# An encoder in split float32 products: streamed operands and low weights get start places of their own

## The chip, the cores and the metric

The kernel runs on one core of a Trainium2 chip. The metric is the device time of one execution in microseconds (us); smaller is better. Engines are named as in the profile: PE is the matrix engine (TensorE) and PEld its weight loads, DVE is VectorE, ACT is ScalarE, POOL is GpSimd, and SP issues DMAs.

## The reference

The kernel computes two layers of an encoder on 16 learned and 256 input tokens (272 together) of width 2048. All tensors are float32. Cut to what matters:

```python
for i in range(DEPTH):                                   # 2 layers
    h = _rmsnorm(h_stream, norm_mix[i])
    proj = h @ w_in[i]                                   # 2048 -> q 1024, k 256, v 256, f 1024, gates 2 x 2048
    ...                                                  # q, k: per-head norm and rotary; sigmoid of the gates
    a_br = attn @ w_attn_br[i]                           # 8 heads of 128, 2 key/value heads -> 2048
    s_br = fr.reshape(B, L, FOURIER_WIDTH) @ w_four[i]   # real part of a 2-D DFT of f -> 2048
    merged = g_attn * a_br + g_four * s_br
    h_stream = h_stream + merged @ w_out[i]
    h2 = _rmsnorm(h_stream, norm_ffn[i])
    up = h2 @ w_up[i]                                    # 2048 -> gate 5632 and value 5632
    u_gate = _dwconv3_centred(up[..., :D_FF], w_conv[i], b_conv[i])
    h_stream = h_stream + (jax.nn.silu(u_gate) * up[..., D_FF:]) @ w_down[i]
return h_stream[:, N_META:]
```

## The kernel before

Activations lie transposed: 128 channels across the partitions, the tokens along the row. Every large product is made of three matmuls in a reduced float32 format: an operand x is kept as a high half (x rounded) and a low half (x minus the high half), weights likewise, and the sum is high weights times high x, high weights times low x, low weights times high x. In the function `group` these are L248, L249 and L250, in this order, each with a 128 x 128 block of weights that is loaded anew, and the tokens as the stream. A stream has 272 columns in layer 0. In layer 1 some tokens are not needed any more: most streams have 258 columns (`lo` is 14), those of the up-value and down products 256 (`lo2` is 16). There two streams of 256 fit one result buffer, so high and low x go through in a single instruction of 512 columns (L244), followed by low weights times high x with 256 (L245); the last group of the last down product is done in the three-matmul form.

`order` is a list of all products by key (layer, kind, number): f, k, v, q (input projections), ga, gf (gates), s (Fourier branch), a (attention branch), o (output), ug and uv (the up product's gate and value half), d (down). Each product's weights come in chunks of 4 x 2 blocks, 512 KB, through SP's queue into `raw`, four buffers. `split_w` makes of each chunk the high weights `wh` on ACT (L193) and the low weights `wl` on DVE (L196), three buffers each. `group` asks for chunks two ahead; the work of the other engines is written between the matmuls by `step` and `pump`. The tile framework adds the semaphores.

Streams come from few tiles: `xHL` (the normalised residual, 16 rows of channels, high and low beside each other), `qH` and `qL`, `mH` and `mL` (the gated sum that goes to `w_out`), and `gHL` (the FFN's inner activations). Their rows are 320 words long (`XP`), more than the 272 in use, and the tokens begin at a word that the table in L50 gives, by tile and layer:

```python
X_AT, Q_AT, G_AT = (8, 24), (24, 40), (40, 48)
```

The high and the low half of a tile begin at the same word. In this text the place of an operand is the number of its first 4-byte word within its partition, modulo 64, as the built program lays it out; words skipped by `lo` count. Since 320 is five times 64, it is the same for all rows of a tile. Before the change:

| products | stream | place, high and low | place of `wh`, `wl` |
|---|---|---|---|
| layer 0: f, k, v, q, ga, gf, a, o, ug, uv, d | 272 | 8, 8 | 32, 32 |
| layer 1: f, k, v | 272 | 24, 24 | 32, 32 |
| layer 1: q, ga, gf, a, o, ug | 258 | 38, 38 | 32, 32 |
| layer 1: uv | 512 and 256 | 40, 40 | 32, 32 |
| layer 1: d | 512 and 256 | 32, 32 | 32, 32 |

Of the kernel before, what the change touches and what calls it, by code (L numbers as in the profile page):

```python
# [11 lines left out]
F32R = mybir.dt.float32r  # L12
# [4 lines left out]
P = 128  # L17
# [3 lines left out]
T = NM + SEQ  # L21
# [3 lines left out]
NH = 8  # L25
# [7 lines left out]
CW = 4  # L33
MG = 2
FF_SPLIT = (24, 20)
PRE = 26
XP = 320
# [9 lines left out]
HC = 64  # L47
HC1 = HC + 1
TH = T // 2 + 2
X_AT, Q_AT, G_AT = (8, 24), (24, 40), (40, 48)  # L50
BLK = ((0, 16), (16, 144), (144, 272))

C_COS, C_SIN, C_MASK = 0, T, 2 * T
# [58 lines left out]
def encoder_kernel(ctx, tc, xT, params, consts, bmat, w_in, w_abr, w_four, w_f64, w_out, w_up, w_down, outT):  # L112
    nc = tc.nc
    per = ctx.enter_context(tc.tile_pool(name="per", bufs=1))
    wp = ctx.enter_context(tc.tile_pool(name="wp", bufs=3))
# [4 lines left out]
    order = []  # L120
# [25 lines left out]
            k0 += n  # L146
    chunks = [ch for _, chs in order for ch in chs]
    folded = {i for i, k in enumerate(k for k, chs in order for _ in chs) if k[1] == "s"}
    st = {"raw": 0, "fetch": 0, "next": 0, "grp": 0}
    raws, splits, behind = {}, {}, {}  # L150
    RAW, LOOK = 4, 2
# [34 lines left out]

    def split_w(i, a, b, eng=None):
        if i not in splits:
            splits[i] = tuple(wp.tile([P, CW, MG * P], F32R, tag=t, name=f"{t}{i}") for t in ("wh", "wl"))
        h, lo = splits[i]  # L190
        r = raws[i]
        if eng is None:
            nc.scalar.copy(h[:, a:b], r[:, a:b])  # L193
        else:
            eng.tensor_copy(h[:, a:b], r[:, a:b])
        nc.vector.tensor_tensor(lo[:, a:b], r[:, a:b], h[:, a:b].bitcast(F32), op=ALU.subtract)  # L196
        if b == CW:
            del raws[i]
# [185 lines left out]
    nc.gpsimd.memset(remO, 0.0)  # L384

    def xs(k, half, lo=0, l=0):
        return xHL[:, k, half, X_AT[l] + lo:X_AT[l] + T]

    cos = cst[:, C_COS:C_COS + T]
    sin = cst[:, C_SIN:C_SIN + T]  # L390
# [58 lines left out]
    for l in range(DEPTH):  # L449
        last = l == DEPTH - 1  # L450
        lo = 14 if last else 0
# [5 lines left out]
        with tc.tile_pool(name=f"mix{l}", bufs=1) as mp:  # L457
            x64 = mp.tile([96, TH], F32R, name="x64")
            E = mp.tile([P, NH, XP], F32, tag="q1", name="E")[:, :, 0:T]
            qL = mp.tile([P, NH, XP], F32R, name="qL")[:, :, Q_AT[l]:Q_AT[l] + T]  # L460
            AHn = 3 * 4 * T
            ALn = 8 * XP
            o1Hf = mp.tile([P, AHn], F32R, tag="aH", name="o1H")
# [233 lines left out]
            cnt = [0]  # L697
            for pn in pns:
                nc.gpsimd.memset(pn[:, 0:P], 0.0)
            qH = mp.tile([P, NH, XP], F32R, tag="q1", name="qH")[:, :, Q_AT[l]:Q_AT[l] + T]  # L700

            def q_stage(i, qp, qsq):
                kv, j = i // 2, i % 2
# [147 lines left out]
            for half in range(2):  # L851
                mH = mL = None
                for kind, i in BRANCH_ORDER[half]:
                    j = i - 4 * half
                    if kind == "ga":
                        tha[i] = gate("ga", i)
                    elif kind == "gf":
                        w64s.append(split_w64(l, i))
                        thf[i] = gate("gf", i)
                    elif kind == "s":  # L860
                        def s_evac(m, ps, th=thf[i]):
                            e, o = (mp.tile([P, TH], F32, tag=t, name=t) for t in ("se", "so"))
                            for a, p_ in ((e, ps[0]), (o, ps[1])):
                                nc.scalar.copy(a, p_[:, TH:2 * TH])
                                nc.vector.tensor_tensor(a, p_[:, :TH], a, op=ALU.add)
                            sp = mp.tile([P, T], F32, tag="sp", name="sp", bufs=2)
                            nc.vector.tensor_tensor(sp[:, 0:TH], e, o, op=ALU.add)
                            nc.vector.tensor_tensor(sp[:, TH:T], e[:, T - TH:0:-1], o[:, T - TH:0:-1], op=ALU.subtract)
                            t_ = th[:, m, lo:T]
                            nc.vector.scalar_tensor_tensor(t_, t_, 1.0, sp[:, lo:T], op0=ALU.add, op1=ALU.mult)  # L870

                        four_group((l, "s", i), fr, x64, w64s.pop(0), s_evac)
                    else:
                        if mH is None:
                            drain()
                            mHf = mp.tile([P, AHn], F32R, tag="aH", name="mH")
                            mLf = mp.tile([P, ALn], F32R, tag="aL", name="mL")
                            mH, mL = (t_[:, :8 * XP].rearrange("p (k t) -> p k t", k=8)[:, :, Q_AT[l]:Q_AT[l] + T] for t_ in (mHf, mLf))
                        ps = group((l, "a", i), lambda kt: (qH[:, kt, lo:T], qL[:, kt, lo:T]), W)
                        for m in range(MG):  # L880
                            k = 2 * j + m
                            t_, h_ = tha[i][:, m, lo:T], mH[:, k, lo:T]
                            nc.vector.scalar_tensor_tensor(t_, t_, 1.0, ps[m][:, :W], op0=ALU.add, op1=ALU.mult)
                            nc.vector.tensor_tensor(t_, t_, thf[i][:, m, lo:T], op=ALU.add)
                            nc.scalar.copy(h_, t_)
                            nc.vector.tensor_tensor(mL[:, k, lo:T], t_, h_.bitcast(F32), op=ALU.subtract)
                for mg in range(8):
                    ps = group((l, "o", half, mg), lambda kt: (mH[:, kt, lo:T], mL[:, kt, lo:T]), W)
                    for m in range(MG):
                        mt = 2 * mg + m  # L890
                        nc.vector.scalar_tensor_tensor(XT[:, mt, lo:T], ps[m][:, :W], 0.5, XT[:, mt, lo:T], op0=ALU.mult, op1=ALU.add)
                        if half == 1:
                            norm_in(mt, P_NF + l * KT)


        with tc.tile_pool(name=f"ffn{l}", bufs=1) as fp:
            hold = {}
            push(norm_stats(hold), 8)
            fused = 2 * W2 <= 512
            k0 = 0  # L900
            for c, n in enumerate(FF_SPLIT):
                gHL = fp.tile([P, FF_SPLIT[0], 2, XP], F32R, tag="gHL", name="gHL")[:, :, :, G_AT[l]:G_AT[l] + T]
                gH, gL = gHL[:, :, 0, :], gHL[:, :, 1, :]
                for i in range(k0 // MG, (k0 + n) // MG):
                    ps = group((l, "ug", i), xr(lo), W)
                    drain()
                    cs = []
                    for m in range(MG):
                        mt = 2 * i + m
                        wc = lambda t: prm[:, P_CW + (l * 3 + t) * FT + mt:P_CW + (l * 3 + t) * FT + mt + 1]  # L910
                        bc = prm[:, P_CB + l * FT + mt:P_CB + l * FT + mt + 1]
                        u = fp.tile([P, T], F32, tag="u", name="u", bufs=3)
                        nc.vector.tensor_tensor(u[:, lo:T], ps[m][:, :W], rstdB[:, lo:T], op=ALU.mult)
                        cv = fp.tile([P, T], F32, tag="cv", name="cv", bufs=4)
                        nc.scalar.activation(cv[:, lo2:T], u[:, lo2:T], AF.Identity, bias=bc, scale=wc(1))
                        a = max(lo2, 1)
                        nc.vector.scalar_tensor_tensor(cv[:, a:T], u[:, a - 1:T - 1], wc(0), cv[:, a:T], op0=ALU.mult, op1=ALU.add)
                        nc.vector.scalar_tensor_tensor(cv[:, lo2:T - 1], u[:, lo2 + 1:T], wc(2), cv[:, lo2:T - 1], op0=ALU.mult, op1=ALU.add)
                        nc.scalar.activation(cv[:, lo2:T], cv[:, lo2:T], AF.Silu)
                        nc.vector.tensor_tensor(cv[:, lo2:T], cv[:, lo2:T], rstdB[:, lo2:T], op=ALU.mult)  # L920
                        cs.append(cv)
                    ps = group((l, "uv", i), (lambda kt: (xHL[:, kt, :, X_AT[l] + lo2:X_AT[l] + T],)) if fused else xr(lo2), W2)
                    for m in range(MG):
                        j = 2 * i + m - k0
                        cv = cs[m]
                        val = ps[m][:, :W2]
                        if fused:
                            v = fp.tile([P, W2], F32, tag="v", name="v", bufs=2)
                            nc.scalar.copy(v, ps[m][:, W2:2 * W2])
                            nc.vector.tensor_tensor(v, v, val, op=ALU.add)  # L930
                            val = v
                        nc.vector.tensor_tensor(cv[:, lo2:T], cv[:, lo2:T], val, op=ALU.mult)
                        nc.scalar.copy(gH[:, j, lo2:T], cv[:, lo2:T])
                        nc.vector.tensor_tensor(gL[:, j, lo2:T], cv[:, lo2:T], gH[:, j, lo2:T].bitcast(F32), op=ALU.subtract)
                lastc = c == len(FF_SPLIT) - 1
                for mg in range(8):
                    two = fused and not (lastc and mg == 7)
                    ps = group((l, "d", c, mg), (lambda kt: (gHL[:, kt, :, lo2:T],)) if two
                               else (lambda kt: (gH[:, kt, lo2:T], gL[:, kt, lo2:T])), W2)
                    for m in range(MG):  # L940
                        mt = 2 * mg + m
# [62 lines left out]
```

## Time and profile before

| | |
|---|---|
| median of 3 runs | 2562.33 us (2560.87 to 2563.58) |
| the profiled execution | 2561.68 us, of which the span is 2559.8 us |
| granted clock of TensorE | 0.999 of full speed |
| PE busy | 2552.6 us, 19732 matmuls |
| DVE, ACT busy | 1690.4 us, 1211.4 us |
| DMA | 465 MB, 182 GB/s |

Matmuls overlap, and their ends are modelled: one of 272 columns is shown as 285 ns long, although the next one starts well before. What counts is the step from one start to the next. It is had from the count of matmuls in a stretch of time in which only one kind runs, or from the start times in the timeline. In a row of the windows the numbers are: the stretch, its length, PE's busy time with the count, the granted clock, the share of DMA, and GB/s. A count takes in the two matmuls that began before the stretch and still run at its start. In the timeline a row has start and length in us, then engine, line, operation, result and operands, shape. A group's row has its count, its busy time, the mean length in ns, and the idle time ahead of it.

### The profile page before, as it was taken

What the parts mean: (1) busy time and instruction counts of PE and PEld (TensorE: products, weight loads), DVE (VectorE), ACT (ScalarE), POOL (GpSimd) and SP (SyncE); (2) the same over time, 40 slices, a digit from 0 to 9 for tenths busy, and PEclk for the clock granted to TensorE, in tenths of its full rate; (3) what the DMA queues carried; (4) which work ended last, traced back from release to release, by engine and by line L of the source; (5) the groups of instructions that cost most, each with busy time, mean ns of one, the idle gap of its engine ahead of it and who ended that gap; (6) DMA issues with size and microseconds to landing.
All of it is one profiled execution on the core that took longest, in us unless ns stands there. A gap on an engine that the chain in (4) does not pass through costs nothing.

```text
span 2559.8 us, 47859 instructions
## 1 busy us (share of the span) xinstructions
PE 2552.6 (100%) x19732; PEld 2494.2 (97%) x19732; DVE 1690.4 (66%) x2691; ACT 1211.4 (47%) x1741; POOL 18.3 (1%) x37
## 2 busy tenths in 40 slices
PE   9999999999999999999999999999999999999999
PEld 9999999999999999999999999999999998999988
DVE  7687767766565446655566878677766665566654
ACT  6455434554444334444444555345554543455443
POOL 0000000000000000000000000000000000000000
PEclk9999999999999999999999999999999999999999
DMA  7555656555555555555554546666555556655565
GB/s 236 166 153 166 192 183 189 185 175 179 180 176 181 177 178 181 175 181 178 177 172 153 174 150 199 192 199 191 184 186 189 185 187 190 189 188 186 186 202 160
DMA packets 132011, 465.34 MB, mean 182 GB/s; under 512 B 15312, under 2 KB 19280, under 8 KB 131792
## 3 DMA queue, kind: packets, MB, share of 16 engines
q1 hardware_dynamic: 127424, 457.37, 56.5%
q10 hardware_dynamic: 4368, 4.92, 0.6%
q8 instruction: 154, 2.52, 0.4%
q14 instruction: 65, 0.53, 0.1%
HBM read 457.35 MB, written 2.10 MB: 179 GB/s over the span
## 4 chain that ended last, share of the span: by engine, by line
PE 98%; DVE 1%; DMA 0%; ACT 0%; issue 0%; SPq 0%; DVEq 0%; ACTq 0%
PE ps_ug L249 7%; PE ps_ug L248 7%; PE ps_ug L250 7%; PE ps_uv L244 6%; PE ps_d L244 6%; PE ps_d L249 4%; PE ps_d L250 4%; PE ps_d L248 4%; PE ps_uv L248 3%; PE ps_uv L249 3%; PE ps_uv L250 3%; PE ps_uv L245 3%; PE ps_d L245 3%; PE ps_o L249 2%; PE ps_o L248 2%; PE ps_gf L248 2%
## 5 line engine op out<-in xcount | busy, mean ns | idle before, releaser
L196 DVE TENSOR_TENSOR wl<-raw,wh 128x1024 fp32r<-128x1024 f32 (+1 forms) x835 | 1016.8, 1220 | 697.3 <-ACT wh L193 692.4
L193 ACT CAST wh<-raw 128x1024 fp32r<-128x1024 f32 (+1 forms) x834 | 871.3, 1047 | 994.4 <-PE ps_ug L249 159.5
L248 PE MATMUL ps_ug<-xHL,wh 128*128 128x272 f32 (+1 forms) x1408 | 399.6, 284 | 0.0
L249 PE MATMUL ps_ug<-xHL,wh 128*128 128x272 f32 (+1 forms) x1408 | 399.0, 283 | 0.0
L250 PE MATMUL ps_ug<-xHL,wl 128*128 128x272 f32 (+1 forms) x1408 | 399.0, 283 | 0.0
L248 PEld LDWEIGHTS ps_ug<-xHL,wh 128*128 128x128 f32 x1408 | 264.2, 188 | 0.9
L249 PEld LDWEIGHTS ps_ug<-xHL,wh 128*128 128x128 f32 x1408 | 264.2, 188 | 0.1
L250 PEld LDWEIGHTS ps_ug<-xHL,wl 128*128 128x128 f32 x1408 | 264.1, 188 | 0.0
L244 PE MATMUL ps_uv<-xHL,wh 128*128 128x512 f32 x704 | 245.0, 390 | 0.0
L244 PE MATMUL ps_d<-gHL,wh 128*128 128x512 f32 x664 | 230.3, 391 | 0.0
L249 PE MATMUL ps_d<-gHL,wh 128*128 128x272 f32 (+1 forms) x744 | 212.0, 285 | 0.0
L248 PE MATMUL ps_d<-gHL,wh 128*128 128x272 f32 (+1 forms) x744 | 212.0, 285 | 0.0
L250 PE MATMUL ps_d<-gHL,wl 128*128 128x272 f32 (+1 forms) x744 | 212.0, 285 | 0.0
L248 PE MATMUL ps_uv<-xHL,wh 128*128 128x272 f32 x704 | 200.6, 285 | 0.0
L249 PE MATMUL ps_uv<-xHL,wh 128*128 128x272 f32 x704 | 200.6, 285 | 0.0
L250 PE MATMUL ps_uv<-xHL,wl 128*128 128x272 f32 x704 | 200.6, 285 | 0.0
L245 PE MATMUL ps_uv<-xHL,wl 128*128 128x256 f32 x704 | 198.5, 282 | 0.0
L245 PE MATMUL ps_d<-gHL,wl 128*128 128x256 f32 x664 | 185.9, 280 | 0.0
L244 PEld LDWEIGHTS ps_uv<-xHL,wh 128*128 128x128 f32 x704 | 132.1, 188 | 26.9
L244 PEld LDWEIGHTS ps_d<-gHL,wh 128*128 128x128 f32 x664 | 124.2, 187 | 27.2
L248 PE MATMUL ps_ga<-xHL,wh 128*128 128x272 f32 (+1 forms) x512 | 147.5, 288 | 0.0
L248 PE MATMUL ps_gf<-xHL,wh 128*128 128x272 f32 (+1 forms) x512 | 146.3, 286 | 0.0
(284 smaller groups left out, 5891.7 us busy)
## 6 DMA issues: line engine op xcount, KB each, us to landing
raw<-in_w_up SPq DMA_DIRECT2D x352, 512.0 KB, 3.5
raw<-in_w_in SPq DMA_DIRECT2D x207, 512.0 KB, 3.6
raw<-in_w_down SPq DMA_DIRECT2D x176, 512.0 KB, 3.5
raw<-in_w_out SPq DMA_DIRECT2D x64, 512.0 KB, 3.5
raw<-in_w_four SPq DMA_DIRECT2D x32, 512.0 KB, 3.7
raw<-in_w_abr SPq DMA_DIRECT2D x32, 512.0 KB, 3.5
qs<-qp ACTq DMA_DIRECT2D x32, 68.0 KB, 4.1
outT<-ot ACTq DMA_DIRECT2D x16, 128.0 KB, 4.0
```

Source lines behind the costliest of these rows:

```text
L193: nc.scalar.copy(h[:, a:b], r[:, a:b])
L196: nc.vector.tensor_tensor(lo[:, a:b], r[:, a:b], h[:, a:b].bitcast(F32), op=ALU.subtract)
L244: nc.tensor.matmul(o2, h[:, c, sl], ab, start=kt == 0, stop=False)
L245: nc.tensor.matmul(o, lo[:, c, sl], ab[:, 0, :], start=False, stop=kt == nk - 1)
L248: nc.tensor.matmul(o, h[:, c, sl], a, start=kt == 0, stop=False)
L249: nc.tensor.matmul(o, h[:, c, sl], b, start=False, stop=False)
L250: nc.tensor.matmul(o, lo[:, c, sl], a, start=False, stop=kt == nk - 1)
```

## The change

The start words become pairs, one for the high and one for the low half, by tile and layer. The low weights get a tile that is 64 words longer, and for the down product of both layers they begin 16 words into it. The fused streams of layer 1 (L244) now read two stretches that need not be 320 words apart: in uv they are 296 words apart. The program's instructions, their order on every engine and their waits stay as they are; only addresses, and the distance between the two parts of that fused stream, differ.

```diff
-X_AT, Q_AT, G_AT = (8, 24), (24, 40), (40, 48)
+X_AT, Q_AT, G_AT = ((4, 28), (24, 0)), ((20, 44), (40, 16)), ((12, 28), (0, 0))
+WL_AT = {(0, "d"): 16, (1, "d"): 16}
...
+    wl_at = [WL_AT.get(k[:2], 0) for k, chs in order for _ in chs]
...
     def split_w(i, a, b, eng=None):
         if i not in splits:
-            splits[i] = tuple(wp.tile([P, CW, MG * P], F32R, tag=t, name=f"{t}{i}") for t in ("wh", "wl"))
+            h = wp.tile([P, CW, MG * P], F32R, tag="wh", name=f"wh{i}")
+            lo = wp.tile([P, CW * MG * P + 64], F32R, tag="wl", name=f"wl{i}")
+            o = wl_at[i]
+            splits[i] = h, lo[:, o:o + CW * MG * P].rearrange("p (c m) -> p c m", c=CW)
...
     def xs(k, half, lo=0, l=0):
-        return xHL[:, k, half, X_AT[l] + lo:X_AT[l] + T]
+        return xHL[:, k, half, X_AT[l][half] + lo:X_AT[l][half] + T]
...
-            qL = mp.tile([P, NH, XP], F32R, name="qL")[:, :, Q_AT[l]:Q_AT[l] + T]
+            qL = mp.tile([P, NH, XP], F32R, name="qL")[:, :, Q_AT[l][1]:Q_AT[l][1] + T]
...
-            qH = mp.tile([P, NH, XP], F32R, tag="q1", name="qH")[:, :, Q_AT[l]:Q_AT[l] + T]
+            qH = mp.tile([P, NH, XP], F32R, tag="q1", name="qH")[:, :, Q_AT[l][0]:Q_AT[l][0] + T]
...
-                            mH, mL = (t_[:, :8 * XP].rearrange("p (k t) -> p k t", k=8)[:, :, Q_AT[l]:Q_AT[l] + T] for t_ in (mHf, mLf))
+                            mH, mL = (t_[:, :8 * XP].rearrange("p (k t) -> p k t", k=8)[:, :, o:o + T] for t_, o in zip((mHf, mLf), Q_AT[l]))
...
+            def both(t_, k, at):
+                a, n = at[0] + lo2, XP + at[1] - at[0]
+                if n == XP:
+                    return t_[:, k, :, a:a + W2]
+                return t_[:, k].rearrange("p r n -> p (r n)")[:, a:a + 2 * n].rearrange("p (r n) -> p r n", r=2)[:, :, :W2]
...
-                gHL = fp.tile([P, FF_SPLIT[0], 2, XP], F32R, tag="gHL", name="gHL")[:, :, :, G_AT[l]:G_AT[l] + T]
-                gH, gL = gHL[:, :, 0, :], gHL[:, :, 1, :]
+                gHL = fp.tile([P, FF_SPLIT[0], 2, XP], F32R, tag="gHL", name="gHL")
+                gH, gL = (gHL[:, :, e, G_AT[l][e]:G_AT[l][e] + T] for e in range(2))
...
-                    ps = group((l, "uv", i), (lambda kt: (xHL[:, kt, :, X_AT[l] + lo2:X_AT[l] + T],)) if fused else xr(lo2), W2)
+                    ps = group((l, "uv", i), (lambda kt: (both(xHL, kt, X_AT[l]),)) if fused else xr(lo2), W2)
...
-                    ps = group((l, "d", c, mg), (lambda kt: (gHL[:, kt, :, lo2:T],)) if two
+                    ps = group((l, "d", c, mg), (lambda kt: (both(gHL, kt, G_AT[l]),)) if two
```

The places that come of it:

| products | stream | place, high and low | place of `wh`, `wl` |
|---|---|---|---|
| layer 0: f, k, v, q, ga, gf, a, o, ug, uv | 272 | 4, 28 | 32, 32 |
| layer 0: d | 272 | 44, 60 | 32, 48 |
| layer 1: f, k, v | 272 | 24, 0 | 32, 32 |
| layer 1: q, ga, gf, a, o, ug | 258 | 38, 14 | 32, 32 |
| layer 1: uv | 512 and 256 | 40, 16 | 32, 32 |
| layer 1: d | 512 and 256 | 48, 48 | 32, 48 |

## Prediction, made before the run

> **What bounds the kernel now.** I read the page's busy line first, then the chain that ended last, then who waited for whom on TensorE.
>
> ```profile
> span 2559.8 us, 47859 instructions
> PE 2552.6 (100%) x19732; PEld 2494.2 (97%) x19732; DVE 1690.4 (66%) x2691; ACT 1211.4 (47%) x1741; POOL 18.3 (1%) x37
> PE 98%; DVE 1%; DMA 0%; ACT 0%; issue 0%; SPq 0%; DVEq 0%; ACTq 0%
> PE ps_f L304 <- ACT wh L193: 1.8, 2, 0.9
> PE ps_idle L364 <- DVE ones L360: 1.1, 1, 1.1
> ```
>
> TensorE is the whole chain (98%), and its longest wait on anything sums to 1.8 us. Nothing can be hidden better here: the time is the number of matmuls times the step from one start to the next. The busy durations do not show that step, because matmuls overlap. I take it from counts in pure windows and from start times.
>
> ```profile
> 560.00:800.00 240.00, 240.00 (x1948) 1.00 0.57 178
> 820.00:940.00 120.00, 120.00 (x975) 1.00 0.56 177
> 1772.00:1812.00 40.00, 40.00 (x339) 1.00 0.58 183
> 2090.00:2210.00 120.00, 120.00 (x694) 1.00 0.61 191
> ```
>
> These are stretches of one stage each, TensorE alone: length, busy time, count, granted clock, DMA share, GB/s. Two of each count had begun before the window. Layer 0's up products (first row) step by 240/1946 = 123.3 ns, and its down product by 120/973 = 123.3, both at 272 columns. Layer 1's output product (third row, 258 columns) steps by 40/337 = 118.7. Layer 1's down product (fourth row) issues a 512-column and a 256-column stream in turn: 120/346 = 346.8 ns a pair. The granted clock is 1.00 throughout.
>
> Now start times, for stages too short or too mixed for a window.
>
> ```profile
> 1999.63 0.28 PE L249 MATMUL ps_ug<-xHL,wh 128*128 128x258 f32 x1
> ...
> 2001.19 0.28 PE L250 MATMUL ps_ug<-xHL,wl 128*128 128x258 f32 x1
> 1383.74 0.29 PE L248 MATMUL ps_v<-xHL,wh 128*128 128x272 f32 x1
> ...
> 1384.88 0.29 PE L248 MATMUL ps_v<-xHL,wh 128*128 128x272 f32 x1
> 2547.73 0.28 PE L248 MATMUL ps_d<-gHL,wh 128*128 128x256 f32 x1
> ...
> 2550.97 0.28 PE L248 MATMUL ps_d<-gHL,wh 128*128 128x256 f32 x1
> 1899.89 0.39 PE L244 MATMUL ps_uv<-xHL,wh 128*128 128x512 f32 x1
> 1900.12 0.28 PE L245 MATMUL ps_uv<-xHL,wl 128*128 128x256 f32 x1
> 1900.23 0.39 PE L244 MATMUL ps_uv<-xHL,wh 128*128 128x512 f32 x1
> ...
> 1900.93 0.39 PE L244 MATMUL ps_uv<-xHL,wh 128*128 128x512 f32 x1
> ```
>
> Layer 1's up-gate product: 13 steps in 1.56 us, 120.0 ns. Layer 1's v: 9 steps in 1.14 us, 126.7. The last group of the last down product: 27 steps in 3.24 us, 120.0. Layer 1's up-value pair: three in 1.04 us, 346.7.
>
> Three of these speak for placement. The place of an operand (its first word, modulo 64) is 8 for every wide stream of layer 0 and 24 in layer 1's v, with the weights' place 32 in both. Width and instruction are the same, the clock too, and the step is 123.3 against 126.7. Layer 1's output and up-gate products, 118.7 and 120.0, have equal width and equal places, so the place alone does not decide; what the previous matmul left matters too. And uv's 256-column stream takes 0.11 us behind a 512-column one (1900.12 to 1900.23), while d's last group, at another place, needs 120.0 ns for the same width. So a step of this kernel moves by up to 3.4 ns with no change of work, and that is the scale of everything below.
>
> What could couple the two is the weight load that runs under each stream.
>
> ```profile
> 700.05 0.29 PE L248 MATMUL ps_ug<-xHL,wh 128*128 128x272 f32 x1
> 700.06 0.19 PEld L249 LDWEIGHTS ps_ug<-xHL,wh 128*128 128x128 f32 x1
> ...
> 700.18 0.28 PE L249 MATMUL ps_ug<-xHL,wh 128*128 128x272 f32 x1
> 700.18 0.19 PEld L250 LDWEIGHTS ps_ug<-xHL,wl 128*128 128x128 f32 x1
> ```
>
> The stream of L248 (high half) runs while high weights load, and that of L249 (low half) while low weights load. That is why separate places for the halves and for the low weights can matter at all.
>
> **The change, part by part.** It adds no instruction, no wait and no byte of traffic. What it moves are start addresses, so each part is a count times a change of step. The counts come from the groups kept apart by shape.
>
> ```profile
> L248 PE MATMUL ps_ug<-xHL,wh 128*128 128x272 f32 x704 | 200.9, 285 | 0.0
> L248 PE MATMUL ps_uv<-xHL,wh 128*128 128x272 f32 x704 | 200.6, 285 | 0.0
> L248 PE MATMUL ps_d<-gHL,wh 128*128 128x272 f32 x704 | 200.6, 285 | 0.0
> L248 PE MATMUL ps_ga<-xHL,wh 128*128 128x272 f32 x256 | 74.4, 291 | 0.0
> L248 PE MATMUL ps_q<-xHL,wh 128*128 128x272 f32 x128 | 37.2, 291 | 0.0
> L248 PE MATMUL ps_ug<-xHL,wh 128*128 128x258 f32 x704 | 198.6, 282 | 0.0
> L244 PE MATMUL ps_uv<-xHL,wh 128*128 128x512 f32 x704 | 245.0, 390 | 0.0
> L244 PE MATMUL ps_d<-gHL,wh 128*128 128x512 f32 x664 | 230.3, 391 | 0.0
> ```
>
> - A, layer 0, 272 columns: ug, uv, d with 704 per line, ga, gf, o with 256, q and a with 128, three lines each: 3 x (2112 + 768 + 256) = 9408 matmuls, 1160 us at 123.3. Places before: 8 for both halves. After: 4 high and 28 low, and in d 44 and 60 with low weights at 48 instead of 32.
> - B, layer 1, 258 columns: ug 704 and the same five smaller products, 3 x (704 + 768 + 256) = 5184 matmuls, at 118.7 to 120.0 some 618 us. The high half stays at 38; the low one goes from 38 to 14.
> - C, layer 1, pairs: 704 + 664 = 1368, 474 us. In uv the low part of the stream goes from 40 to 16; in d both go from 32 to 48 and the low weights with them.
> - D, layer 1's f, k and v: only the 192 low streams move, 24 to 0.
>
> No row shows the new places, so each step is bounded from both sides by what placing has been seen to do. For A the nearest rows are 123.3 (place 8) and 126.7 (place 24, four words from the new 28). The upper bound is +3.4 ns on all, +32 us. For the lower one I take the same distance on the other side, -3.4 ns, -32 us. The estimate between them: a pair moves 768 columns in 346.7 ns, 0.451 ns a column, by which 272 columns take 122.8 and 258 take 116.5. A stands 0.5 ns over that, B 2.2 to 3.5 ns. By the pairs' rate A could give 5 us and B 2112 x 3.5 + 3072 x 2.2 = 14 us. I take 1.5 ns for A, between the pairs' 0.5 and the 3.4 of the bound: 14 us. For B I take half of its surplus, 1.5 ns: 8 us; its bounds are +1.3 ns on the 3072 that step by 118.7 (+4 us) and -3.5 ns on all (-18 us). For C I take nothing, with bounds of 3.4 ns on each of the two streams of a pair, 1368 x 6.8 = 9 us either way: uv at place 40 and d at place 32 have the same 346.7, so the pair has shown no taste. For D 192 x 3.4 = 0.7 us either way, taken as nothing.
>
> Writes at the new places cost nothing that counts:
>
> ```profile
> L196 DVE TENSOR_TENSOR wl<-raw,wh 128x1024 fp32r<-128x1024 f32 (+1 forms) x835 | 1016.8, 1220 | 697.3 <-ACT wh L193 692.4
> ```
>
> A chunk of weights feeds 24 matmuls, 2.96 us at 123.3; its split on VectorE takes 1.22 us. Cover would be gone only if that write more than doubled, and then all 835 chunks would be late.
>
> Sum: -14 - 8 = -22 us. The profiled execution took 2561.7 us, 1.9 more than its span, and the median of the runs is 0.7 above that: 2561.7 - 22 + 0.7 = 2540.
>
> [...]
>
> **The rivals.**
>
> *Slower: the low halves land badly.* In layer 0 the low streams go to 28, while the only row near it, layer 1's v at 24, has 126.7. If the low streams alone go there, 3136 x 3.4 = +11 us; if they drag the high streams of the same sequence with them, +32. Middle: 2583. It decides as soon as a third of A loses 3.4 ns and B gives back under 11 us. Against it: in v the high halves stand at 24 as well, with high weights under them, and high places 4 and 44 keep off that.
>
> *No change.* The place does not matter, and 118.7 against 120.0 at equal places shows that the differences are patterns a stage falls into. For it: uv and d, at places 40 and 32, have equal pairs. Against it: 123.3 and 126.7 hold through whole stages. Then 2562. The Trainium skill, "SBUF — State Buffer", section "Who interferes with whom", says that TensorE's two read ports, for streams and for weights, are independent and that it waits on no one; by that rule this rival holds, and the two steps of one width speak against it.
>
> *Much faster.* Each stage finds a place as much better than its own as 8 is than 24: A -32, B -18, C -9: 2503. Nothing shows such a step, nor that it can't be.
>
> **How the numbers follow.** My forecast, some gain between 6 and 45 us, gets 0.59: steps have slack in B and two levels in A, and the halves get places against the weights that load under them. Much faster gets 0.09, no change 0.09, slower 0.23, since A holds half the time and its only neighbouring row is worse. A measurement here can tell about 0.2%, 5 us, from no change. Faster: 0.68; same: 0.09; slower: 0.23. The likeliest is 2540. Where A, B and C all lie at their upper bounds the time is 2562 + 32 + 4 + 9 = 2607, at their lower ones 2503. I cut the upper end to 2590, which holds all of A at 126.7 with the rest unchanged to within 4 us, and set the lower end at 2500, so that about 1.5 in 10 is left out. Forecast alone: 2517 to 2556.
>
> **What would show it.** Counts and waits must be as before, and TensorE still the chain. Right: the window in layer 0's up products holds about 120/0.1218 matmuls in 120 us (985, not 973), layer 1's up-gate steps by 118.5 or less, and pairs stay within 3 ns of 346.7. Wrong: A steps by 123.3 or more, or gains sit in C, or a new wait of TensorE on the splits of L193 and L196 appears.

## The result, and the profile after

| | before | after |
|---|---|---|
| median | 2561.97 us (2560.87 to 2563.58, 4 runs) | 2587.02 us (2583.68 to 2587.36, 4 runs) |
| profiled execution | 2561.68 us, span 2559.8 us | 2587.07 us, span 2585.2 us |
| granted clock | 0.999 | 1.000 |

The changed kernel takes 1.0094 times as long (95% interval 1.0077 to 1.0112): 25 us slower, where 22 us faster was forecast. The page after has the same instructions and the same waits. These are its busy line, its chain, the two longest waits of TensorE, and the row for the split of the weights:

```profile
span 2585.2 us, 47859 instructions
PE 2577.6 (100%) x19732; PEld 2520.4 (97%) x19732; DVE 1689.5 (65%) x2691; ACT 1211.4 (47%) x1741; POOL 18.3 (1%) x37
PE 99%; DVE 1%; DMA 0%; issue 0%; ACT 0%; SPq 0%; DVEq 0%
PE ps_f L309 <- ACT wh L198: 2.0, 4, 0.7
PE ps_idle L369 <- DVE ones L365: 1.1, 1, 1.1
L201 DVE TENSOR_TENSOR wl<-raw,wh 128x1024 fp32r<-128x1024 f32 (+1 forms) x835 | 1016.9, 1220 | 720.5 <-ACT wh L198 713.7
```

TensorE is still the whole chain, waits on nothing for more than 2 us in sum, and the write of `wl` at its new place takes 1220 ns as before. So the 25 us lies in the steps between matmuls. The lines of `group` are now L253, L254, L255 (were L248 to L250), and L249 and L250 for the pairs (were L244 and L245). The windows after, with two matmuls of each count begun before the window:

```profile
560.00:800.00 240.00, 240.00 (x1897) 1.00 0.52 174
840.00:960.00 120.00, 120.00 (x966) 1.00 0.52 176
980.00:1190.00 210.00, 210.00 (x1690) 1.00 0.53 176
1800.00:1836.00 36.00, 36.00 (x296) 1.00 0.55 185
2120.00:2240.00 120.00, 120.00 (x708) 1.00 0.57 193
```

Layer 0's first run of up products: 240/1895 = 126.7 ns a step, from 123.3. Its down product: 120/964 = 124.5. Its second run of up products, same operands and places as the first: 210/1688 = 124.4. Layer 1's output product: 36/294 = 122.4, from 118.7. Layer 1's down product: 120/353 = 339.9 ns a pair (340.0 by start times), from 346.8; the only stage that gained as a whole. A stage of 126.7 and one of 124.4 with nothing different between them, not even a place, is the row that the experiments had to explain.

How the loss builds up is had from the first matmul of each stage in the timeline. Before:

```profile
526.46 0.28 PE L248 MATMUL ps_ug<-xHL,wh 128*128 128x272 f32 x1
811.43 0.28 PE L248 MATMUL ps_d<-gHL,wh 128*128 128x272 f32 x1
1308.71 0.29 PE L248 MATMUL ps_f<-xHL,wh 128*128 128x272 f32 x1
1813.60 0.28 PE L248 MATMUL ps_ug<-xHL,wh 128*128 128x258 f32 x1
2085.65 0.39 PE L244 MATMUL ps_d<-gHL,wh 128*128 128x512 f32 x1
2218.77 0.28 PE L248 MATMUL ps_ug<-xHL,wh 128*128 128x258 f32 x1
2444.91 0.39 PE L244 MATMUL ps_d<-gHL,wh 128*128 128x512 f32 x1
```

And after:

```profile
532.88 0.29 PE L253 MATMUL ps_ug<-xHL,wh 128*128 128x272 f32 x1
825.50 0.28 PE L253 MATMUL ps_d<-gHL,wh 128*128 128x272 f32 x1
1327.25 0.28 PE L253 MATMUL ps_f<-xHL,wh 128*128 128x272 f32 x1
1839.55 0.28 PE L253 MATMUL ps_ug<-xHL,wh 128*128 128x258 f32 x1
2114.22 0.39 PE L249 MATMUL ps_d<-gHL,wh 128*128 128x512 f32 x1
2244.79 0.28 PE L253 MATMUL ps_ug<-xHL,wh 128*128 128x258 f32 x1
2472.42 0.39 PE L249 MATMUL ps_d<-gHL,wh 128*128 128x512 f32 x1
```

The differences are +6.4, +14.1, +18.5, +26.0, +28.6, +26.0 and +27.5 us, and +25.4 at the end of the span. Layer 0 costs 18.5; layer 1's products of 258 columns 7.4 ahead of the up product and, together with the fused up-value products, 2.6 and 1.5 in its two runs; the two down products of layer 1 give back 2.6 and 2.1.

Now single steps. In the slow stretch of layer 0, in the up-value product of the changed kernel:

```profile
699.72 0.29 PE L253 MATMUL ps_uv<-xHL,wh 128*128 128x272 f32 x1
...
700.10 0.29 PE L253 MATMUL ps_uv<-xHL,wh 128*128 128x272 f32 x1
...
700.48 0.29 PE L253 MATMUL ps_uv<-xHL,wh 128*128 128x272 f32 x1
...
700.86 0.29 PE L253 MATMUL ps_uv<-xHL,wh 128*128 128x272 f32 x1
```

Three steps take 0.38 us; the trace's start times, which have nanoseconds, split it into 128 after L253, 124 after L254 and 128 after L255. The steps of 128 follow the two high streams; the low stream at place 28 steps by 124. The same three matmuls, at the same places, in the same execution, in layer 0's f:

```profile
38.16 0.29 PE L253 MATMUL ps_f<-xHL,wh 128*128 128x272 f32 x1
...
40.00 0.29 PE L253 MATMUL ps_f<-xHL,wh 128*128 128x272 f32 x1
40.12 0.28 PE L254 MATMUL ps_f<-xHL,wh 128*128 128x272 f32 x1
40.24 0.28 PE L255 MATMUL ps_f<-xHL,wl 128*128 128x272 f32 x1
40.36 0.29 PE L253 MATMUL ps_f<-xHL,wh 128*128 128x272 f32 x1
```

Six sequences from 38.16 to 40.36: 2.20/18 = 122.2 ns a step, split as 124, 123, 120. So one set of places has a faster and a slower pattern of steps, and the kernel sat in the slower one from about 240 us to the down product at 825.5.

Layer 1 shows it more strongly. Two neighbouring groups of its up-gate product in the changed kernel, number 12, which starts at 2244.79 (shown above), and number 13:

```profile
2255.89 0.39 PE L249 MATMUL ps_uv<-xHL,wh 128*128 128x512 f32 x1
...
2266.98 0.29 PE L253 MATMUL ps_ug<-xHL,wh 128*128 128x258 f32 x1
...
2278.71 0.40 PE L249 MATMUL ps_uv<-xHL,wh 128*128 128x512 f32 x1
```

Group 12 takes 11.10 us for its 96 matmuls, 115.6 ns a step; group 13 takes 11.73 us, 122.2. The operands' places are the same. Before the change these groups step by 120.0. Only one other whole group of layer 1, of q at 1426 us, ran at 115.6.

### The profile page after: what moved, and what is told of

Its sections match the earlier page's. It is cut to its first block, busy times and chain, and to the rows that moved or that the text cites. A ratio compares the mean times of both kernels' runs of the same rounds, so it can differ in the third digit from the quotient of the medians.

```text
span 2585.2 us, 47859 instructions
## 1 busy us (share of the span) xinstructions
PE 2577.6 (100%) x19732; PEld 2520.4 (97%) x19732; DVE 1689.5 (65%) x2691; ACT 1211.4 (47%) x1741; POOL 18.3 (1%) x37
## 4 chain that ended last, share of the span: by engine, by line
PE 99%; DVE 1%; DMA 0%; issue 0%; ACT 0%; SPq 0%; DVEq 0%
PE ps_ug L253 7%; PE ps_ug L255 7%; PE ps_ug L254 7%; PE ps_uv L249 6%; PE ps_d L249 6%; PE ps_d L255 4%; PE ps_d L254 4%; PE ps_d L253 4%; PE ps_uv L253 3%; PE ps_uv L255 3%; PE ps_uv L254 3%; PE ps_uv L250 3%; PE ps_d L250 3%; PE ps_gf L253 2%; PE ps_o L253 2%; PE ps_o L255 2%
## 5 line engine op out<-in xcount | busy, mean ns | idle before, releaser
L201 DVE TENSOR_TENSOR wl<-raw,wh 128x1024 fp32r<-128x1024 f32 (+1 forms) x835 | 1016.9, 1220 | 720.5 <-ACT wh L198 713.7
L253 PE MATMUL ps_ug<-xHL,wh 128*128 128x272 f32 (+1 forms) x1408 | 404.0, 287 | 0.0
L255 PE MATMUL ps_ug<-xHL,wl 128*128 128x272 f32 (+1 forms) x1408 | 403.9, 287 | 0.0
L254 PE MATMUL ps_ug<-xHL,wh 128*128 128x272 f32 (+1 forms) x1408 | 401.4, 285 | 0.0
L253 PEld LDWEIGHTS ps_ug<-xHL,wh 128*128 128x128 f32 x1408 | 267.5, 190 | 0.9
L255 PEld LDWEIGHTS ps_ug<-xHL,wl 128*128 128x128 f32 x1408 | 264.5, 188 | 0.0
L254 PEld LDWEIGHTS ps_ug<-xHL,wh 128*128 128x128 f32 x1408 | 264.1, 188 | 0.1
L249 PE MATMUL ps_uv<-xHL,wh 128*128 128x512 f32 x704 | 245.1, 391 | 0.0
L249 PE MATMUL ps_d<-gHL,wh 128*128 128x512 f32 x664 | 225.9, 389 | 0.0
L255 PE MATMUL ps_d<-gHL,wl 128*128 128x272 f32 (+1 forms) x744 | 213.7, 287 | 0.0
L254 PE MATMUL ps_d<-gHL,wh 128*128 128x272 f32 (+1 forms) x744 | 213.3, 287 | 0.0
L253 PE MATMUL ps_d<-gHL,wh 128*128 128x272 f32 (+1 forms) x744 | 211.8, 285 | 0.0
L253 PE MATMUL ps_uv<-xHL,wh 128*128 128x272 f32 x704 | 203.1, 288 | 0.0
L255 PE MATMUL ps_uv<-xHL,wl 128*128 128x272 f32 x704 | 203.0, 288 | 0.0
L254 PE MATMUL ps_uv<-xHL,wh 128*128 128x272 f32 x704 | 201.7, 286 | 0.0
L250 PE MATMUL ps_uv<-xHL,wl 128*128 128x256 f32 x704 | 198.3, 282 | 0.0
L250 PE MATMUL ps_d<-gHL,wl 128*128 128x256 f32 x664 | 183.3, 276 | 0.0
L249 PEld LDWEIGHTS ps_uv<-xHL,wh 128*128 128x128 f32 x704 | 132.0, 188 | 27.3
L249 PEld LDWEIGHTS ps_d<-gHL,wh 128*128 128x128 f32 x664 | 124.6, 188 | 25.8
L253 PE MATMUL ps_ga<-xHL,wh 128*128 128x272 f32 (+1 forms) x512 | 148.8, 291 | 0.0
L253 PE MATMUL ps_gf<-xHL,wh 128*128 128x272 f32 (+1 forms) x512 | 147.9, 289 | 0.0
```

Of the source, the lines that this page charges most:

```text
L249: nc.tensor.matmul(o2, h[:, c, sl], ab, start=kt == 0, stop=False)
L250: nc.tensor.matmul(o, lo[:, c, sl], ab[:, 0, :], start=False, stop=kt == nk - 1)
L253: nc.tensor.matmul(o, h[:, c, sl], a, start=kt == 0, stop=False)
L254: nc.tensor.matmul(o, h[:, c, sl], b, start=False, stop=False)
L255: nc.tensor.matmul(o, lo[:, c, sl], a, start=False, stop=kt == nk - 1)
```

## Experiments

Two theories went in. **P**: the places fix the step; the new places of A and B are slower, that of layer 1's d faster. **S**: the places only fix which patterns are possible; which of them holds is set by how a stage starts or is interrupted, and it then stays. By S the same kernel may run faster with a disturbance added. Beside these stood the possibility that the longer `wl` tile costs something by itself. The kernels compute the whole result; where matmuls are added, their result is not used.

**Only the longer tile.** All start words as before, `wl` 64 words longer:

```diff
-X_AT, Q_AT, G_AT = ((4, 28), (24, 0)), ((20, 44), (40, 16)), ((12, 28), (0, 0))
-WL_AT = {(0, "d"): 16, (1, "d"): 16}
+X_AT, Q_AT, G_AT = ((8, 8), (24, 24)), ((24, 24), (40, 40)), ((40, 40), (48, 48))
+WL_AT = {}
```

> All start words as before the change; only the tile of the low weights is 64 words longer, so two of its three buffers lie elsewhere. Both theories: no stage moves, 2562 us within 3. Rival (the padding itself costs, not the places): layer 0's wide streams step by 126.7 ns instead of 123.3 and the time goes to 2580 or more.

2562.20 us (10 runs), ratio to the kernel before 1.0002 (0.9993 to 1.0012). The longer tile costs at most some 3 us by that interval; the rest of the 25 us is left to the starts.

**Only layer 1's d.**

```diff
+X_AT, Q_AT, G_AT = ((8, 8), (24, 24)), ((24, 24), (40, 40)), ((40, 40), (0, 0))
+WL_AT = {(1, 'd'): 16}
```

> Of the change only layer 1's down product: both halves at place 48, its low weights at 48. Theory P (the places fix the pace): its pair falls from 346.7 to 340.0 ns as in the changed kernel, 664 x 6.7 = 4.4 us, all else as before: 2557.5 us. Theory S (places allow several stable patterns, and what interrupts a stage decides which one holds): the same pair, since in the changed kernel it holds through all 16 groups, so 2557 to 2558. Rival: the 340.0 needs the other stages' new places too; then 2562.

2557.15 us (10 runs), ratio 0.9983 (0.9973 to 0.9992): 4.6 us faster. Its window in d:

```profile
2090.00:2210.00 120.00, 120.00 (x708) 1.00 0.61 193
```

120/353 = 339.9 ns a pair, as in the changed kernel. This part is a gain of its own.

**Only layer 0.**

```diff
+X_AT, Q_AT, G_AT = ((4, 28), (24, 24)), ((20, 44), (40, 40)), ((12, 28), (48, 48))
+WL_AT = {(0, 'd'): 16}
```

> Of the change only layer 0: high halves at 4, low at 28, in d 44 and 60 with the low weights at 48. Both theories: layer 0's wide streams as in the changed kernel, 126.7 ns in most groups, +20 us: 2582. P needs every group of equal places at one step. S expects groups at 122.3 and groups at 126.7 again, the early f, k, v and ga among the first, and the share of each to be open: 2575 to 2585.

2580.56 us (4 runs), ratio 1.0075 (1.006 to 1.009): +18.8 us, the 18.5 that the starts gave for layer 0. The up window again has 126.7 ns a step (1897 matmuls in 240 us). It does not tell P from S.

**A disturbance of growing size.** The changed kernel with one extra matmul ahead of every up-gate group, of 16 columns at group 0 and 4 more at each group:

```diff
+                    pk = psum.tile([P, 512], F32, tag="aux", name="ps_kick")
+                    nk = 16 + 4 * i
+                    nc.tensor.matmul(pk[:, :nk], BH[:, 0, :P], BH[:, 0, :nk], start=True, stop=True)
                     ps = group((l, "ug", i), xr(lo), W)
```

> The changed kernel with one extra matmul ahead of each of the 22 up-gate groups of both layers, 16 + 4 i columns wide for group i, its result unused: 44 short interruptions of different length, some 0.1 us each, 5 us together. P: the steps inside all groups stay, 126.7 ns in layer 0's up products and 122.0 in layer 1's; 2592 us. S: after some of the kicks layer 0's up products (ug and the uv behind it) run at 122.3 ns instead of 126.7, after others at 126.7; each stretch of 192 that flips gives 0.83 us; with half of the 22 flipped 2583.

2591.29 us in one run. By the total alone this looks like P. The groups say otherwise. Windows of layer 0's groups 12, 13 and 14, 15, 16:

```profile
972.00:994.00 22.00, 22.00 (x175) 1.00 0.57 182
996.00:1041.00 45.00, 45.00 (x371) 1.00 0.59 181
1043.00:1065.00 22.00, 22.00 (x176) 1.00 0.54 175
1068.00:1089.00 21.00, 21.00 (x175) 1.00 0.58 182
```

127.2, 122.0, 126.4 and 121.4 ns. Up to 60 columns (groups 0 to 11) the 126.7 stays. Group 12, behind 64 columns, has 126.7 as well, where the changed kernel had 124.4. The 68 columns ahead of group 13 turn the stage to the faster pattern, which group 14 keeps, and later ones turn it back and forth (group steps 126.65 and 122.2 to 122.4 by the start times, without the first step behind the extra matmul). Same operands, same places, and a step that one small matmul changes: P falls in its simple form. S missed the time because only 6 of layer 0's 22 groups ran in the faster pattern, and because 4 of the 10 groups behind the first down product ran at 126.7, where the changed kernel had 124.4.

**The same 152 disturbances in three layouts, and a scan of the weights' place.** To see which patterns a set of places has, an extra matmul of 64 to 136 columns stands ahead of each ug, uv, d and o group of both layers:

```diff
+    def next_kick():
+        kick(64 + 4 * (kicks[0] % 19))
+        kicks[0] += 1
```

In the changed kernel:

> The changed kernel with an extra matmul, result unused, ahead of every ug, uv, d and o group of both layers, 152 in all, its width going through 64, 68, ... 136 columns again and again; some 0.11 us each, 17 us together. P (places fix the pace): steps as without, layer 0's up products 126.7 ns, 2604 us. S (several stable patterns at the same places): in layer 0's ug, uv and o the groups stand at 122.2, 124.4 or 126.7, the width deciding; about half of the 60 groups at 122.2, and 2590 us or less. Layer 0's d and layer 1's ug and o should show a second value as well.

2598.52 us, one run. Windows in groups 2 and 3 of layer 0's up-gate product:

```profile
583.00:594.00 11.00, 11.00 (x92) 1.00 0.60 191
606.50:617.50 11.00, 11.00 (x89) 1.00 0.63 188
```

11/90 = 122.2 and 11/87 = 126.4. Over layer 0's ug, uv and o, 26 of 60 groups ran at 122.2 and 33 at 126.7 (one was interrupted); d had 9 at 122.2 and 7 at 124.4. In ug, uv and o, 68, 80, 92, 124 and 132 columns turned slow to fast each time, 64, 88 and 108 to 120 left slow as it was (108 also turned fast to slow once), and 76, 84, 128 and 136 turned fast to slow. Since the widths come in a fixed cycle, each met nearly the same pattern every time: what the width does and what the pattern ahead does are not told apart. Layer 1's d had 340.0 (11 groups) and 350.0 (4), and one output group of layer 1, behind 72 columns, ran at 115.6.

In the kernel before:

> The same extra matmuls in the kernel with all start words as before the change (low weights' tile padded). P: 123.3 ns in all of layer 0, 2562 + 17 = 2579 us. S: layer 0 shows a second value beside 123.3, and layer 1's ug and o go between 118.7 and 120.0 by the width. If 123.3 is the only pattern there, equal places have one pattern and unequal ones several, and the before kernel owes its time to that; if it has worse ones too, before was in a good one.

2579.17 us, one run; 152 extra matmuls at some 0.11 us account for the 17 us over the kernel with the longer tile. A window in one group:

```profile
600.50:612.00 11.50, 11.50 (x95) 1.00 0.58 182
```

11.5/93 = 123.7, as near as so short a stretch gives it. By start times, without the first step behind the extra matmul, the groups of layer 0's up products have means of 123.4 to 123.8, and the second half of every disturbed group of layer 0 has 123.3. The equal halves at place 8 came back to a single pattern under all 76 extra matmuls of layer 0. That fits the 123.3 of all its long stages before. Layer 1 of the same run is different, although its halves are equal too: its up-gate and output groups have 118.7 or 120.0, and its down groups 346.7 (6 of 15) or 353.3 (9). Equal halves do not make a single pattern by themselves.

With the streams of before, no extra matmuls, and the weights' place varied by group:

> Streams as before the change (layer 0 at 8, layer 1 at 38 and 40), but the weights' place goes by group: in ug group i high and low weights at 32 + 4 i for i below 16, in uv the high weights alone; from 16 on the low weights alone at 40, 48, 56, 72, 80, 88. P: each place has its own step, between 120 and 130 ns in layer 0, the same in ug and uv groups of equal places, and layer 1's uv pair takes 340.0 where stream and weights lie as in the changed down product (16 words apart for the high weights, 0 for the low). S: values come from a few multiples (122.2, 123.3, 124.4, 126.7) and depend on the group ahead as well.

2571.59 us, one run. Layer 0's up-gate groups ran at 123.3 or 123.4 (group 0 with the weights left at 32, groups 3 and 14 with them at 44 and 24) to 126.7 (groups 2, 13 and 15), none below 123.3. Weights at 36 under a stream at 8 gave 126.6 (group 1). So the weights' place counts, which a single stream address cannot show. Each place was seen in one group, so its other patterns, if it has any, are not known.

With equal halves at other places (layer 0 at 4 and 4, layer 1 at 14 and 14, d at 48 and 48 with weights left at 32):

> Equal halves at other places, with the 152 extra matmuls of the scans: layer 0 at 4 and 4 (d too), layer 1's 258 columns at 14 and 14, uv at 16, d at 48 with the low weights left at 32. If several patterns come from unequal halves, layer 0 has a single value in all groups, whatever it is (near 123.3), and layer 1's 258 columns a value or two, not 122.2. If they come from the places 4 and 28 as such, layer 0 shows two values here as well. For d: 340.0 if the streams' place makes it, 346.7 or 353.3 if it needs the low weights at 48.

2599.24 us, one run.

```profile
604.60:616.00 11.40, 11.40 (x94) 1.00 0.56 185
```

11.4/92 = 123.9 in this window; by start times, without the first step behind the extra matmul, 124.3 to 124.6 in all 76 groups of layer 0's ug, uv, o and d. Again one pattern, but a slower one than at place 8. Here the streams stand at 4 with the weights at 32, the distance that streams at 8 had to weights at 36, and 124.4 is not 126.6: the distance alone does not decide either. d kept 353.3 or 348.9 with its streams at 48 and its low weights at 32: its 340.0 needs the low weights at 48 too.

**Four matmuls.** Extra matmuls only where S would put the changed kernel's layer 0 into its faster patterns:

```diff
+                    if (l, i) in ((0, 1), (0, 12)):
+                        kick(68 if i == 1 else 104)
                     ps = group((l, "ug", i), xr(lo), W)
...
+                    if l == 0 and mg == 0:
+                        kick(72)
```

> The changed kernel with four extra matmuls in all, results unused, in layer 0: ahead of ug group 1 (68 columns), of each of the two runs of d groups (72), and of ug group 12 (104), widths behind which the scan had the fast pattern. S: ug and uv run at 122.2 ns instead of 126.7 for 43 groups of 96, -18.3 us, d at 122.2 instead of 124.4, 2112 x 2.2 = -4.7 us: 2564. P: four matmuls more, 0.4 us: 2587.

2570.13 us (5 runs), ratio to the kernel before 1.0031 (1.002 to 1.0043), 16.9 us under the changed kernel. The first of the four in the timeline, and the window that was 126.7:

```profile
557.61 0.29 PE L255 MATMUL ps_uv<-xHL,wl 128*128 128x272 f32 x1
557.73 0.19 PE L347 MATMUL ps_kick<-BH 128*128 128x68 f32 x1
557.76 0.37 PE L253 MATMUL ps_ug<-xHL,wh 128*128 128x272 f32 x1
557.97 0.29 PE L254 MATMUL ps_ug<-xHL,wh 128*128 128x272 f32 x1
```

```profile
560.00:800.00 240.00, 240.00 (x1966) 1.00 0.58 179
```

240/1964 = 122.2 ns, held for more than 240 us after one matmul of 68 columns. This is the main proof of S: more work, less time. Of the 6 us missed against the expectation some 4 lie in the second run of up products, which was already at 124.4 in the changed kernel, where 126.7 had been assumed: 20 groups of 96 by 2.2 ns.

**Only layer 1's low halves.**

```diff
+X_AT, Q_AT, G_AT = ((8, 8), (24, 0)), ((24, 24), (40, 16)), ((40, 40), (48, 48))
+WL_AT = {}
```

> Of the change only the low halves of layer 1's q, k, v, f, ga, gf, a, o, ug and uv streams (38 to 14, 24 to 0, in uv 40 to 16). P and S: the 258-column streams at 122.2 ns instead of 118.7 and 120.0, the uv pair 346.7, +12 us: 2573 to 2574. Rival: the loss of layer 1 comes in with layer 0's pattern; then 2562.

2574.14 us (4 runs), ratio 1.0051 (1.0036 to 1.0065): +12.4 us. Its window in layer 1's output product has 40/328 = 122.0 ns:

```profile
1784.00:1824.00 40.00, 40.00 (x330) 1.00 0.59 184
```

The three parts add up: 18.8 + 12.4 - 4.6 = 26.6 us, against 25.0 measured together.

**Two attempts at a kernel that beats both.** First the changed layer 0 with 24 extra matmuls (68 columns ahead of the first o groups, the a groups and the later gates, besides those above), layer 1 as before but for d:

```diff
+X_AT, Q_AT, G_AT = ((4, 28), (24, 24)), ((20, 44), (40, 40)), ((12, 28), (0, 0))
...
+                        if l == 0:
+                            kick(68)
```

> A version out of the parts: layer 0 at the changed places, layer 1 as before but for its d (both halves and low weights at 48), and an extra matmul ahead of layer 0's later gate, a and first o groups (68 columns) and at the four places of the kernel with four. S: layer 0's wide streams at 122.2 in nearly all groups from 250 us on, 1.1 ns under before, about -9 us; some 25 extra matmuls +2.5; early layer 0 +1.5; layer 1's d -4.4: 2552, under the 2557 of the kernel with layer 1's d alone. P: 2577.

Median 2567.74 us, ratio 1.0024 (0.9999 to 1.0049), and the median hides the finding: of 12 executions, six took 2555.34 to 2557.52 us and six 2577.96 to 2580.28. The profiled one took 2555.92 and has 122.2 ns in the up window. That the other six fell into the slower pattern fits in size (layer 0's ug and uv, 4224 matmuls at 126.7 instead of 122.2, and d, 2112 at 124.4 instead of 122.2, would make 19 + 5 us), but none of them was profiled, so it is argued and not shown. As a kernel this is no gain that one can count on, and even the faster six lie 4 us over the 2552 expected.

Then equal halves and no extra matmuls: layer 0 as before, layer 1's d as changed, and in layer 1 all weights of q, ga, gf, a, o and ug at place 0 instead of 32:

```diff
+    def w_at(k):
+        if k[0] == 0:
+            return 0, 0
+        return {"d": (0, 16), "uv": (0, 0), "s": (0, 0)}.get(k[1], (32, 32) if k[1] in ("q", "ga", "gf", "a", "o", "ug") else (0, 0))
```

> No extra matmuls and equal halves everywhere: layer 0 as before the change; layer 1's d with both halves and its low weights at 48; and in layer 1's q, ga, gf, a, o and ug both kinds of weights at place 0 instead of 32, which in the scan of places gave 117.8 ns in three of three groups (8, 10 and 13 there are the neighbours 0, 8, 20; 8 is this one). If equal halves have one pattern for a place, 258 columns run at 117.8 instead of 120.0 (2112 matmuls of ug, -4.7 us) and 118.7 (3072 others, -2.8), with d's -4.4: 2550. If the 117.8 hung on what stood ahead in the scan, only d's gain is left: 2557.

2556.16 us (11 runs), ratio 0.9979 (0.997 to 0.9988), 5.3 us under the kernel before, all eleven within 2.7 us. By its median it is the fastest kernel of the study, with the d-only one level with it within the intervals. Its windows in the first and the second run of layer 1's output product:

```profile
1616.00:1648.00 32.00, 32.00 (x274) 1.00 0.56 187
1771.00:1807.00 36.00, 36.00 (x299) 1.00 0.54 188
```

32/272 = 117.6 and 36/297 = 121.2 ns: two patterns at equal halves too, the faster one below the 118.7 of before, the slower one above it. The expectation was missed by 6 us: by start times about two thirds of the matmuls of q, ga, gf, a and o (1800 of the 2766 in stretches long enough to tell) ran in the slower one, 3.3 ns over the faster.

## Why the prediction was wrong

- **What bounds the kernel** was right: TensorE's steps are the time, no wait came or went, the writes cost nothing, counts are equal.
- **A is the step that failed.** The prediction took 1.5 ns as a gain, on the ground that A stands 0.5 ns over the pairs' rate a column and that bounds of 3.4 ns lie on both sides. No row of the trace before showed a long stage of this width under 123.3, so neither the size nor the sign had one behind it. The new places turned out to have 122.2, 124.4 and 126.7 where the old ones had 123.3: even the fastest gives 1.1 ns, not 1.5, and the kernel ran at 126.7 and 124.4 from about 240 us on. Layer 0 lost 18.5 us, about 2.0 ns on 9408 matmuls, within the bound of +3.4. (The count leaves out layer 0's f, k and v, 576 matmuls that the change moves too; they came out within 1 us.) The forecast's window check (985 matmuls in 120 us) answers with 1895/2, some 947.
- **B failed the same way**, and its bound as well: nearly all groups ran at 122.2, 3.5 ns above the 118.7 of the output product and 2.2 above the 120.0 of the up-gate product. The upper bound of +1.3 ns came from two rows, 118.7 and 120.0, which were two patterns of one layout and said nothing of another layout. Layer 1 without d lost 11.5 us (7.4 + 2.6 + 1.5), where the forecast had 8 as a gain and +4 as the worst. But the same places have a pattern at 115.6, below the 116.5 of the pairs' rate, and two whole groups ran in it. An estimate from these steps: held there, B would have gained 3072 x 3.1 + 2112 x 4.4 ns, some 19 us. No run tried to hold it there.
- **C** was put at nothing and gave a gain of 4.7 us by the starts, within its bound of 9. All of it is in d, whose places had been moved together with the low weights'. That uv and d had equal 346.7 at two places was read as "no taste"; it was a coincidence of two places.
- **D** and the splits: nothing, as forecast.
- **The rival that came true in time** was the slower one, at 2583 for its middle. Its mechanism did only in part. The steps behind the low streams at 28 took 124 ns; those behind the high streams, at 4, took 128. Place 24 of v as a neighbour of 28 told nothing.
- **The hint was in the prediction.** It read 118.7 against 120.0 at equal places and said that what the previous matmul left matters too. It used this for the rival of no change alone. Its consequence was another: a new layout draws a new set of patterns, and a stage then falls into one of them without anything in the layout preferring the faster. With the old patterns known and the new set unknown, the forecast should have been centred on no gain, with wide ends on both sides. The trace before had the stronger hint, against the prediction's reading that 123.3 and 126.7 hold through whole stages. In layer 1's f, whose streams have one place throughout:

```profile
1328.12 0.29 PE L248 MATMUL ps_f<-xHL,wh 128*128 128x272 f32 x1
...
1337.14 0.29 PE L248 MATMUL ps_f<-xHL,wh 128*128 128x272 f32 x1
1341.05 0.29 PE L248 MATMUL ps_f<-xHL,wh 128*128 128x272 f32 x1
...
1350.17 0.29 PE L248 MATMUL ps_f<-xHL,wh 128*128 128x272 f32 x1
```

The first two rows are 72 steps apart, 9.02 us or 125.3 ns a step; the last two are 72 steps apart as well, 9.12 us or 126.7.
- **A rule of the Trainium skill.** "SBUF — State Buffer", section "Who interferes with whom", has TensorE's two read ports independent. No run here tells what the ports do, but a step that goes from 123.3 to 126.7 when the weights' place alone is moved (the scan of the weights' place), and from 126.7 to 122.2 after one small matmul, is not what a reader would expect of streams and weight loads that do not touch each other.

What stays open: why the patterns have the sums that they have (three steps of layer 0 take 366.7, 370.0, 373.3 or 380.0 ns, which are 110, 111, 112 and 114 times 3.33 ns), which of them a given start selects, and why one program fell into two groups of executions. No run measured the weight load apart from the stream, and the growing disturbance and the scans rest on one execution each.

## What to carry to other kernels

Where TensorE steps back to back, an operand's start address and the weights' start address moved the step by a few per cent here, but a layout has to be judged by all the patterns it can fall into, inside the real kernel, and not by the best step seen. Read the step from counts in pure windows or from start times, stage by stage: equal stages with unequal steps mean several patterns. Prefer a layout that keeps one step under every disturbance that you try (layer 0's place 8 with 123.3 here) over one whose faster pattern is better by 0.9% and whose slower one is worse by 2.7%.

## What was not expected of the hardware

- A matmul sequence has stable patterns that last for hundreds of microseconds, and an extra matmul of 68 columns selected another one; 16 to 60 columns did not. Four such matmuls took 16.9 us off a kernel of 2587.
- Over all layouts and weights' places tried, the step of a whole group went from 122.2 to 127.3 ns for 272 columns, from 115.6 to 123.2 for 258, and from 340.0 to 353.3 for a pair of 512 and 256 columns, at a granted clock of 1.00 in the windows read.
- One program split into two groups of six, 23 us apart.
